# Starting the seven-product column blocks one block earlier in both feed-forward phases

## Chip, core and metric

The kernel runs on one core of a Trainium2 chip. The metric is device time in microseconds (us) of one execution. Of the kernel before there are three runs, with a median of 2231.39 us (2228.88 to 2231.76).

## The reference

One streaming-encoder layer on x of 1024 x 1024 in float32: a feed-forward phase (FFN), a mixer (banded attention beside a gated linear recurrence), and a second FFN. Each is wrapped in a norm, a modulation and a gated residual. What the change touches is the up projection of both FFNs:

```python
def swiglu(h, w_gu, w_down):            # h 1024 x 1024, w_gu 1024 x 5632, w_down 2816 x 1024
    g, u = jnp.split(h @ w_gu, 2, axis=-1)
    return (jax.nn.silu(g) * u) @ w_down
...
x = sandwich(x, ffn1, ...)
x = sandwich(x, mix, ...)
x = sandwich(x, ffn2, ...)
```

## The kernel before, in words

Every float32 matrix product is made of three matmuls on a high part and a low part of both operands (`hi` is a rounded copy made by ScalarE, `lo` the remainder, made by VectorE or GpSimd): hi·hi, hi·lo, lo·hi. One matmul is 128 x 128 weights against 512 moving columns.

**The up projection.** The 2816 columns of the gate and of the up half of `w_gu` are worked in 22 column blocks of 128 (`fb`). There are two ways to do one.

- A *plain* block (`part`, lines 453 to 455, with `cut` for the weights and `finish` for the activation) multiplies gate and up weights with the two halves of the tokens (`sh` 0 and 1), over 8 slices k of the inner dimension: 2 x 2 x 8 x 3 = 96 matmuls, of which one token half takes 48. `finish` reads the two banks (Silu on ScalarE, line 487, and the product with the up half on VectorE, line 488) and stores the result to `act_d` in device memory (line 483).
- A *seven-product* block (`block`, `product`, lines 633 to 635) does the same 2 x 2 x 2 product with seven products instead of eight, each over 4 slices: 7 x 4 x 3 = 84 matmuls. They run in the order 1, 2, 6, 5, 7, 3, 4 (`ORDER`). Products 1, 6, 7, 4 accumulate in one bank, `psX`: ScalarE has to copy the bank away after product 1 (`u`, line 649) before product 6 may go on in it, and after product 6 (`v`, line 656) before product 7 may.

**What a seven-product block needs.** Weights: `mix(fb, i)` builds the operand of product i, from sums on GpSimd (line 611), a high copy on ScalarE (line 623) and a low part on VectorE (line 624). Inside a block, the operands of the next block are made one by one in `after(i)`. Moving data: products 4, 5, 6 take sums over slices of the normed input (`hs`), made once per FFN by the generator `sums`: GpSimd adds high and low parts (`whole`, line 549, two 128 x 1024 adds for each of four slices kk), then seven VectorE instructions per kk (lines 566, 569, 573, 577, and 563 three times) and three ScalarE copies (line 559). One call of `sum_step` does one of its 17 steps. Products 3 and 7 take `differences(kk)` (lines 584 and 585, ScalarE then VectorE), which overwrite the second token half of the high and low input slices 0 to 3, so that no plain block can come after them.

**The order.** PE, VectorE, ScalarE and GpSimd each run their instructions in the order in which this hand-written program issues them; SyncE's loads and stores are placed by the scheduler. Two phases following each other may be interleaved on an engine, while each keeps its own order. `DIRECT` says with which block the seven-product blocks begin: 4 in the first FFN (`sub` 0) and 3 in the second (`sub` 2).

- First FFN: `startup` does blocks 0, 1, 2 plainly, with 16 steps of `sums` in the second token half of blocks 1 and 2. `up_phase(3)` then does block 3 plainly: its weights are cut with the low part on GpSimd, the remaining steps of `sums` are taken, and in its second token half the generator `first_needs` runs one step per k: four operands of block 4 (products 1, 2, 6, 5), four `differences`, and behind the block the other three operands (7, 3, 4).
- Second FFN: `head` does blocks 0 and 1 plainly, at the end of the mixer's output phase, with the steps of `sums` in their second token halves. `up_phase(2)` does block 2 plainly (low part on VectorE) with `first_needs` for block 3.

The temporary 128 x 512 tiles of tag `v` have two buffers (`tv`), shared by `finish` (`a`) and the two running sums of each kk (`hsum`). `raw` has three buffers, `wh` and `wl` four each, `u` three, `t4` 22. Behind the up projection, `down_phase` multiplies pairs of activation blocks with `w_down`; `all_sums` prepares its operands one step per product of a block, reading activations back from device memory for pairs that start below `direct`, and using those kept on the chip for the others.

Of the kernel before, what the change touches and what calls it, by code (L numbers as in the profile page):

```python
# [23 lines left out]
P = 128  # L24
S = 1024
D = 1024
KB = D // P
# [7 lines left out]
NEG = -1e30  # L35
HEAD_WAIT = 8
LATE = 6
FIRST_NEEDS = (1,) * 8
L_WAIT = 11
SHARE = (3, 4, 4, 5, 5)  # L40
LEFT = 40.0
GATES = (2, 0, 2, 4)
NORM_ACT = ()
DIRECT = {0: 4, 2: 3}
KEPT_FROM = 5

FIRST_HALF = (((0, 1), (), ()), ((2, 3), (0,), ()), ((), (1, 2), ()), ((), (3,), (0, 1)), ((), (), (2, 3)))
# [3 lines left out]
def kernel(  # L51
# [32 lines left out]
    def tv(name, shape=(P, 512)):  # L84
        return tmp[0].tile(list(shape), F32, tag="v", bufs=2, name=nm(name))
# [385 lines left out]
    ORDER = (1, 2, 6, 5, 7, 3, 4)  # L471

    def ffn(sub, w_gu, w_down, hh, hl, xin, xout):
# [17 lines left out]
        def load(fb, i):  # L491
            if fb >= NF or (fb, i) in wts or (fb, i) in raws:
                return
            spare = fb == 2 and sub == 0
            shape = [P, KB, P]
            if spare or fb > direct and i == 1:
                raw = t4("sr", F32, shape)
            elif fb == 1 and sub == 0:
                raw = tu("sr", F32, shape)
            else:  # L500
                raw = wpool.tile(shape, F32, tag="raw", bufs=3, name=nm("raw"))
            c0 = i * DFF + fb * P
            nc.sync.dma_start(raw, w_gu[:, c0 : c0 + P].rearrange("(k p) n -> p k n", p=P))
            raws[fb, i] = raw, spare

        def cut(fb, i):
            if (fb, i) not in raws:
                return
            raw, spare = raws.pop((fb, i))
            shape = [P, KB, P]  # L510
            if spare:
                hi, lo = t4("sh", F32R, shape), t4("sl", F32R, shape)
            else:
                hi = wpool.tile(shape, F32R, tag="wh", bufs=4, name=nm("wh"))
# [74 lines left out]
        def sum_step(n=1):  # L589
            for _ in range(n):  # L590
                next(summing, None)
# [12 lines left out]
        def mix(fb, i):  # L604
            if fb >= NF:
                return
            g, u = raws[fb, 0][0], raws[fb, 1][0]
            a, b, c, e = g[:, :4], g[:, 4:], u[:, :4], u[:, 4:]

            def pool(out, p, q, op):  # L610
                nc.gpsimd.tensor_tensor(out, p, q, op=op)  # L611

            if i == 1:
                s1 = first_sum[fb] = tv("wsum", shape=(P, 4, P))
                pool(s1, c, e, ALU.add)
                pool(c, a, c, ALU.subtract)
            s1 = first_sum[fb]
            src = {1: a, 2: b, 6: a, 5: s1, 7: c, 3: b, 4: e}[i]
            if i == 6:
                pool(a, s1, a, ALU.subtract)  # L620
            tag = ("wh", "wl")[ORDER.index(i) % 2]
            t = wpool.tile([P, 2, 4, P], F32R, tag=tag, bufs=4, name=nm("wm"))
            nc.scalar.copy(t[:, 0], src)  # L623
            nc.vector.tensor_tensor(t[:, 1], src, t[:, 0].bitcast(F32), op=ALU.subtract)  # L624
            if i == 6:
                pool(b, b, a, ALU.subtract)
            mixed[fb, i] = t
# [51 lines left out]
        def head():  # L679
            for fb in range(2):  # L680
                for k in range(KB):
                    part(fb, 0, k)
                    yield
                finish(fb, 0)
            for fb in range(2):
                for k in range(KB):
                    part(fb, 1, k)
                    sum_step()
                finish(fb, 1)

        def up_phase(started):

            for fb in range(started, direct):
                for i in range(2):
                    load(fb, i)
                    cut(fb, i)
            for i in range(2):
                load(direct, i)
            for fb in range(started, direct):
                for k in range(KB):  # L700
                    part(fb, 0, k)
                    sum_step()
                finish(fb, 0)

            def first_needs():
                sum_step(100)
                for i in ORDER[:4]:
                    mix(direct, i)
                    yield
                for kk in range(4):  # L710
                    differences(kk)
                    yield
                for i in ORDER[4:]:
                    mix(direct, i)
                    yield

            needs = first_needs()
            for fb in range(started, direct):
                for k in range(KB):
                    part(fb, 1, k)  # L720
                    if fb == direct - 1 and k < len(FIRST_NEEDS):
                        for _ in range(FIRST_NEEDS[k]):
                            next(needs)
                finish(fb, 1)
            for _ in needs:
                pass
            load(direct + 1, 0)
            load(direct + 1, 1)
            for fb in range(direct, NF):

                def after(i):
                    mix(fb + 1, i)
                    next(jobs, None)
                    if i == 3:
                        if next(early, BANK) is BANK and sub == 0:
                            raw_home[0] = "u"
                            bg(1)
                            raw_home[0] = "raw"
                    if fb == NF - 1 and i in ORDER[4:]:
                        units.fetch(ORDER[4:].index(i) + 1)  # L740

                ready[0] = fb
                block(fb, after)
                for i in range(2):
                    raws.pop((fb + 1, i), None)
                    load(fb + 2, i)
            ready[0] = NF
# [216 lines left out]
        def run(make, next_phase=None, started=0):  # L964
# [2 lines left out]
                down_phase(make, next_phase)  # L967

        return SimpleNamespace(
            run=run, load=load, cut=cut, part=part, finish=finish, sum_step=sum_step,  # L970
            fetch_raw=fetch_raw, fetch=fetch, head=head,
        )

# [591 lines left out]
    def startup(f1, hh, hl):  # L1565
# [133 lines left out]
        for k in range(KB):  # L1699
# [5 lines left out]
            if k + 3 < KB:  # L1705
                trans(1, k + 3)
        f1.finish(0, 1)
        for fb in (1, 2):
            for k in range(KB):
                f1.part(fb, 1, k)  # L1710
                f1.sum_step()
            f1.finish(fb, 1)


# [85 lines left out]
```

## Time and profile before

| what | value |
|---|---|
| runs of the kernel before | 2231.39 us median of 3, 2228.88 to 2231.76 |
| the profiled execution | 2231.5 us, its span 2229.6 us |
| mean granted clock of TensorE | 0.993 |
| busy in the span: PE, VectorE (DVE), ScalarE (ACT), GpSimd (POOL) | 97%, 60%, 46%, 34% |

The span runs from the first to the last instruction. In a row of a timeline stand start, duration, engine, line, operation, the tiles written and read, shapes and count; behind it, in brackets, the idle time of that engine just before and what ended it. PE's rows for one matmul show 0.39 us, but matmuls overlap: their starts lie closer together. A row of a table of stages has busy time and number of instructions of each engine, then the granted clock of TensorE, the DMA share and GB/s.

### The profile page before, as it was taken

Reading aid. Unit: us, or ns where it says so; the run is one execution under the profiler, and the core shown is the slowest. Engines: PE = TensorE matmul, PEld = TensorE weight load, DVE = VectorE, ACT = ScalarE, POOL = GpSimd, SP = SyncE. Lnnn points to the kernel's source line nnn. Section 1 sums busy time; section 2 is a strip of 40 time slices with the busy share of each in tenths; the row PEclk is TensorE's granted clock in tenths of the full one; section 3 lists DMA queues with packets and bytes.
Section 4 is the critical chain, followed back from the end, with each engine's and each line's share of the span. In section 5 each row is a group of like instructions: output and inputs, shape, how many; then the busy total and the mean of one; then the engine's idle time right before and its main releaser. Section 6 shows DMA issues by size and latency. Waiting matters only on the chain. (4 is left out here: it accounts for less than half of the span.)

```text
span 2229.6 us, 26752 instructions
## 1 busy us (share of the span) xinstructions
PE 2156.7 (97%) x9963; PEld 1785.0 (80%) x9963; DVE 1332.4 (60%) x1696; ACT 1016.1 (46%) x1567; POOL 758.2 (34%) x538
## 2 busy tenths in 40 slices
PE   5999999999999999999999999999999999999998
PEld 3878788888877788888898988887788788888877
DVE  6686676558356677655336666545866564544456
ACT  3533333334446678721147777436443333334443
POOL 3458885422104111100021120005658793522102
PEclk9999999999999999999999999999999999999999
DMA  9437674459575111166412011464357653348374
GB/s 294 113 120 268 226 272 153 151 183 336 182 240 184 50 50 42 57 221 221 155 40 68 26 55 54 146 199 142 110 181 263 229 209 126 113 155 275 117 230 176
DMA packets 269595, 358.36 MB, mean 161 GB/s; under 512 B 16625, under 2 KB 178585, under 8 KB 269465
## 3 DMA queue, kind: packets, MB, share of 16 engines
q1 hardware_dynamic: 256680, 310.48, 43.0%
q10 hardware_dynamic: 12784, 46.18, 5.4%
q8 instruction: 78, 1.28, 0.2%
q14 instruction: 53, 0.43, 0.1%
HBM read 265.37 MB, written 94.37 MB: 161 GB/s over the span
## 5 line engine op out<-in xcount | busy, mean ns | idle before, releaser
L624 DVE TENSOR_TENSOR wm<-raw,wm 128x512 fp32r<-128x512 f32 x152 | 161.0, 1063 | 165.3 <-ACT wm L623 162.5
L143 ACT CAST dh<-rawd 128x1024 fp32r<-128x1024 f32 x154 | 161.3, 1053 | 212.1 <-PE pv L882 67.0
L144 DVE TENSOR_TENSOR dh<-rawd,dh 128x1024 fp32r<-128x1024 f32 x130 | 161.9, 1250 | 153.4 <-ACT dh L143 145.3
L455 PE MATMUL pj<-hh,wl 128*128 128x512 f32 x576 | 228.3, 396 | 6.3 <-DVE wl L144 4.1
L454 PE MATMUL pj<-hl,wh 128*128 128x512 f32 x576 | 228.5, 397 | 5.7 <-DVE hl L336 5.7
L453 PE MATMUL pj<-hh,wh 128*128 128x512 f32 x576 | 230.9, 401 | 2.8 <-ACT h L344 1.9
L882 PE MATMUL px<-dh,dh 128*128 128x512 f32 x608 | 187.8, 390 | 1.7 <-DVE dh L144 1.7
L882 PE MATMUL pv<-dh,dh 128*128 128x512 f32 x528 | 164.3, 393 | 3.0 <-DVE dh L144 3.0
L325 POOL TENSOR_SCALAR rstd<-rstd 128x1 f32<-128x1 f32 x47 | 31.7, 675 | 392.5 <-ACT junk L324 390.9
L144 POOL TENSOR_TENSOR wl<-raw,wh 128x1024 fp32r<-128x1024 f32 x25 | 61.1, 2450 | 297.8 <-ACT wh L143 252.0
L143 ACT CAST wh<-raw 128x1024 fp32r<-128x1024 f32 (+1 forms) x86 | 86.7, 1010 | 144.9 <-DMA raw<-in_w_in_dram 41.8
L820 POOL TENSOR_TENSOR act<-act,act 128x512 f32<-128x512 f32 x54 | 87.5, 1620 | 158.9 <-DMA act<-act 89.1
L882 PE MATMUL px<-dh 128*128 128x512 f32 x352 | 137.9, 392 | 0.0
L455 PEld LDWEIGHTS pj<-hh,wl 128*128 128x128 f32 x576 | 110.2, 191 | 31.2 <-DVE wl L144 5.7
L882 PEld LDWEIGHTS px<-dh,dh 128*128 128x128 f32 x608 | 113.8, 188 | 26.5 <-DVE dh L144 3.0
L454 PEld LDWEIGHTS pj<-hl,wh 128*128 128x128 f32 x576 | 110.0, 191 | 29.9 <-DVE hl L336 7.6
L453 PEld LDWEIGHTS pj<-hh,wh 128*128 128x128 f32 x576 | 110.2, 191 | 26.2 <-ACT h L344 2.3
L144 DVE TENSOR_TENSOR wl<-raw,wh 128x1024 fp32r<-128x1024 f32 (+1 forms) x61 | 73.9, 1212 | 84.8 <-ACT wh L143 84.8
L633 PE MATMUL psX<-hh,wm 128*128 128x512 f32 x296 | 116.4, 393 | 4.3 <-ACT mixes L656 4.3
L882 PEld LDWEIGHTS pv<-dh,dh 128*128 128x128 f32 x528 | 99.5, 189 | 25.0 <-DVE dh L144 4.3
L633 PE MATMUL psX<-hs,wm 128*128 128x512 f32 x296 | 115.9, 391 | 1.6 <-ACT mixes L649 1.4
L623 ACT CAST wm<-raw 128x512 fp32r<-128x512 f32 x152 | 92.6, 613 | 52.1 <-POOL raw L611 52.0
(311 smaller groups left out, 5783.9 us busy)
## 6 DMA issues: line engine op xcount, KB each, us to landing
rawa<-in_w_ada_dram SPq DMA_DIRECT2D x56, 512.0 KB, 4.5
raw<-in_ffn_w_gu_dram SPq DMA_DIRECT2D x49, 512.0 KB, 4.7
rawd<-acts SPq DMA_DIRECT2D x88, 256.0 KB, 4.3
rawd<-downs SPq DMA_DIRECT2D x88, 256.0 KB, 4.1
raw<-in_w_in_dram SPq DMA_DIRECT2D x44, 512.0 KB, 4.0
sr<-in_ffn_w_gu_dram SPq DMA_DIRECT2D x39, 512.0 KB, 6.3
act<-act SPq DMA_DIRECT2D x37, 512.0 KB, 5.1
acts<-act ACTq DMA_DIRECT2D x36, 512.0 KB, 3.6
```

Source lines behind the costliest of these rows:

```text
L143: nc.scalar.copy(hi, raw)
L144: (eng or nc.vector).tensor_tensor(lo, raw, hi.bitcast(F32), op=ALU.subtract)
L325: nc.gpsimd.tensor_scalar(r, r, eps, None, op0=ALU.add)
L453: nc.tensor.matmul(dst, wh[:, kk, :], xhk[:, sl], start=first, stop=False)
L454: nc.tensor.matmul(dst, wh[:, kk, :], xlk[:, sl], start=False, stop=False)
L455: nc.tensor.matmul(dst, wl[:, kk, :], xhk[:, sl], start=False, stop=last)
L623: nc.scalar.copy(t[:, 0], src)
L624: nc.vector.tensor_tensor(t[:, 1], src, t[:, 0].bitcast(F32), op=ALU.subtract)
L633: nc.tensor.matmul(dst, t[:, 0, kk, :], xh, start=first and kk == 0, stop=False, skip_group_check=True)
L820: nc.gpsimd.tensor_tensor(o, p, q, op=op)
L882: nc.tensor.matmul(dst, a_[:, 0, tk], w_[:, 1, :], start=first and n == 0, stop=last and n == 2, skip_group_check=True,)
```

## The change

- `DIRECT` goes from {0: 4, 2: 3} to {0: 3, 2: 2}. The plain block of `up_phase` is gone in both FFNs: the code for it is deleted. Block 3 of the first FFN and block 2 of the second become seven-product blocks.
- `first_needs` now runs during the last plain block ahead of `up_phase`: in `startup` in the second token half of block 2, in `head` in that of block 1, one step behind each odd k (`need_step`). That gives the operands 1, 2, 6, 5. The other steps (what is left of `sums`, four `differences`, operands 7, 3, 4) are issued at the start of `up_phase`, ahead of the first seven-product block.
- `startup` takes two steps of `sums` per k in the last four k of block 1, so that 20 calls stand ahead of `up_phase` instead of 16. `head` keeps its 16; the call with which `need_step` is paired stands after `sum_step` of the same k.
- The first seven-product block's `wsum` tile moves from tag `v` to tag `u`.
- Its raw weights are loaded ahead of the last plain blocks (in the first FFN they were already loaded there).
- In the second FFN, the pair of blocks 2 and 3 is now kept on the chip for `down_phase`, not read back.

```diff
-FIRST_NEEDS = (1,) * 8
...
-DIRECT = {0: 4, 2: 3}
+DIRECT = {0: 3, 2: 2}
...
-                s1 = first_sum[fb] = tv("wsum", shape=(P, 4, P))
+                s1 = first_sum[fb] = (tu if fb == direct else tv)("wsum", shape=(P, 4, P))
...
+            for i in range(2):
+                load(direct, i)
             for fb in range(2):
                 for k in range(KB):
                     part(fb, 1, k)
                     sum_step()
+                    if fb == 1 and direct == 2:
+                        need_step(k)
                 finish(fb, 1)
 
+
+        def first_needs():
+            for i in ORDER[:4]:
+                mix(direct, i)
+                yield
+            sum_step(100)
+            for kk in range(4):
+                differences(kk)
+                yield
+            for i in ORDER[4:]:
+                mix(direct, i)
+                yield
+
+        needs = first_needs()
+
+        def need_step(k):
+            if k % 2 == 1:
+                next(needs)
+
         def up_phase(started):
 
-            for fb in range(started, direct):
-                for i in range(2):
-                    load(fb, i)
-                    cut(fb, i)
-            for i in range(2):
-                load(direct, i)
-            for fb in range(started, direct):
-                for k in range(KB):
-                    part(fb, 0, k)
-                    sum_step()
-                finish(fb, 0)
-
-            def first_needs():
-                sum_step(100)
-                for i in ORDER[:4]:
-                    mix(direct, i)
-                    yield
-                for kk in range(4):
-                    differences(kk)
-                    yield
-                for i in ORDER[4:]:
-                    mix(direct, i)
-                    yield
-
-            needs = first_needs()
-            for fb in range(started, direct):
-                for k in range(KB):
-                    part(fb, 1, k)
-                    if fb == direct - 1 and k < len(FIRST_NEEDS):
-                        for _ in range(FIRST_NEEDS[k]):
-                            next(needs)
-                finish(fb, 1)
             for _ in needs:
                 pass
             load(direct + 1, 0)
...
         f1.finish(0, 1)
+        for i in range(2):
+            f1.load(3, i)
         for fb in (1, 2):
             for k in range(KB):
                 f1.part(fb, 1, k)
-                f1.sum_step()
+                f1.sum_step(2 if fb == 1 and k >= 4 else 1)
+                if fb == 2:
+                    f1.need_step(k)
             f1.finish(fb, 1)
```

More of the change, by code (lines that the diff above doesn't have):

```diff
@@ L969, in ffn @@
         return SimpleNamespace(
-            run=run, load=load, cut=cut, part=part, finish=finish, sum_step=sum_step,
+            run=run, load=load, cut=cut, part=part, finish=finish, sum_step=sum_step, need_step=need_step,
             fetch_raw=fetch_raw, fetch=fetch, head=head,
```

## The prediction

> **What bounds the kernel now.** I read the page first, then the stages around the heads of the two FFNs, then the timelines of PE, VectorE, GpSimd and ScalarE there.
>
> ```profile
> span 2229.6 us, 26752 instructions
> PE 2156.7 (97%) x9963; PEld 1785.0 (80%) x9963; DVE 1332.4 (60%) x1696; ACT 1016.1 (46%) x1567; POOL 758.2 (34%) x538
> ```
>
> PE is busy for 97% of the span, so fewer matmuls should be time saved, if nothing else becomes late. The price of one matmul, from the chain that ended last:
>
> ```profile
> 2004.27 29.92 PE px L882 x132
> ```
>
> 29.92 / 132 = 0.2267 us from one matmul to the next. A plain block is 96 x 0.2267 = 21.8 us of PE, a seven-product block 84 x 0.2267 = 19.0. The gross gain is 12 matmuls, 2.72 us, in each FFN: 5.4 us in all. But that average hides what the removed block does besides: it covers other engines. The stages show that; columns are PE, weight loads, VectorE, ScalarE, GpSimd, then the clock.
>
> ```profile
> 92.00:116.00 24.00, 24.00 (x108) 19.87 (x107) 16.33 (x8) 4.35 (x6) 21.16 (x8) 1.00 0.19 55
> 116.00:138.00 22.00, 22.00 (x99) 18.22 (x98) 16.89 (x28) 8.11 (x14) 2.98 (x3) 1.00 0.18 61
> 1612.00:1638.00 26.00, 23.55 (x96) 19.03 (x96) 20.95 (x28) 10.02 (x18) 9.14 (x6) 0.93 0.29 91
> ```
>
> The second and third lines are the two blocks that go. PE never waits in the first of them, and VectorE runs 28 instructions in each, for 16.9 and 21.0 us. The change keeps nearly all of these and takes PE's 21.8 us away from over them. So the question is what VectorE still has to do when the last plain block ends.
>
> **First FFN: where VectorE stands.**
>
> ```profile
> 94.58 5.22 POOL L144 TENSOR_TENSOR wl<-raw,wh 128x1024 fp32r<-128x1024 f32 x2 [5.01 <-ACT wh L143]
> 112.91 2.84 POOL L549 TENSOR_TENSOR bot<-hh,hl 128x1024 f32<-128x1024 f32 x1
> 95.64 1.91 DVE L566 TENSOR_TENSOR hsum<-top 128x512 f32<-128x512 f32 x1
> 105.00 2.88 DVE L563 TENSOR_TENSOR hs<-hsum,hs 128x512 fp32r<-128x512 f32 x1
> 116.22 0.68 DVE L563 TENSOR_TENSOR hs<-bot,hs 128x512 fp32r<-128x512 f32 x1
> 116.82 0.68 DVE L566 TENSOR_TENSOR hsum<-top 128x512 f32<-128x512 f32 x1
> 127.98 0.69 DVE L569 TENSOR_TENSOR hsum<-bot,hsum 128x512 f32<-128x512 f32 x1
> 130.40 0.69 DVE L577 TENSOR_TENSOR bot<-bot,top 128x512 f32<-128x512 f32 x1
> 141.33 4.66 DVE L585 TENSOR_TENSOR hl<-bot,hh 128x512 fp32r<-128x512 f32 x4
> 137.68 0.39 PE L633 MATMUL psX<-hh,wm 128*128 128x512 f32 x1
> 144.72 0.50 PE L633 MATMUL psX<-hs,wm 128*128 128x512 f32 x1 [1.44 <-ACT mixes L649]
> 151.30 0.50 PE L633 MATMUL psX<-hh,wm 128*128 128x512 f32 x1 [0.85 <-ACT mixes L656]
> ```
>
> The seven-product blocks start at 137.68, so the last matmul of plain block 2 was due to end at 137.68 - 21.76 = 115.92. At that time VectorE is finishing the sums of the first of four slices (the instruction at 116.22 is the seventh of 28), and the last `z - x` of the sums is at 130.40. While GpSimd adds (until 112.91 + 2.84 = 115.75), a VectorE instruction takes 2.88 us; alone it takes 0.68, and starts follow each other by 0.60 (116.22 and 116.82).
>
> What moves forward: the cut of block 3 is gone, 5.22 us of GpSimd, and with it the wait of 5.01 us that stood ahead of it. In the second FFN, where no cut stands in between, GpSimd went from the first slice straight on:
>
> ```profile
> 1585.65 2.40 POOL L549 TENSOR_TENSOR bot<-hh,hl 128x1024 f32<-128x1024 f32 x1 [4.92 <-DVE hl L336]
> 1588.01 2.85 POOL L549 TENSOR_TENSOR top<-hh,hl 128x1024 f32<-128x1024 f32 x1
> ```
>
> So I take the whole 10.2 us (the other bound is 5.2). The instruction of 116.22 comes at 106.0, and that of 127.98 (the second running sum of the last slice), 11.76 later, at 117.7. One product of `finish` lies in that stretch before and after. Behind it comes `mix` for product 1, which needs that instruction's end (0.69), two copies on ScalarE queued behind each other, and its own 0.68. ScalarE's rows:
>
> ```profile
> 142.54 1.65 ACT L623 CAST wm<-raw 128x512 fp32r<-128x512 f32 x3
> 149.63 0.63 ACT L653 ACTIVATE act<-mixes 128x512 f32<-128x512 f32 x1 [4.44 <-DVE mixes L643]
> 150.17 0.60 ACT L623 CAST wm<-raw 128x512 fp32r<-128x512 f32 x1
> 150.68 0.58 ACT L656 COPY mixes<-psX 128x512 f32<-128x512 f32 x1
> ```
>
> Three copies take 1.65, so two take 1.1: the operand of product 1 is there at 117.7 + 0.69 + 1.1 + 0.68 = 120.2, and PE has been idle since 115.9. This is the wait that the change adds: 4.3 us here, before any disturbance.
>
> It is not the last. Products 1 and 2 take PE 5.4 us; product 6 waits for ScalarE's copy of `psX`, which stands in its queue behind the four `differences` and three weight copies; product 7 waits for the second copy (line 656), behind a Silu that waits for VectorE, whose queue holds four differences, three low parts, one of the next block and the add. That last chain decides. In steps of VectorE: the last `z - x` at 117.7 + 2.42 (as 127.98 to 130.40) + 1.7 (mix 1 and its wait) = 121.8; then it, mix 2, the last low part, mix 6, mix 5 and the product of `finish`, 6 x 0.60 = 3.6: the first difference at 125.5 (rounded up). From the first difference to product 7:
>
> - at least 9 x 0.60 on VectorE + 0.63 + 0.60 + 0.58 on ScalarE = 7.2 us;
> - before, with GpSimd working beside it, 151.30 - 141.33 = 9.97 us.
>
> Then products 7, 3, 4: 36 x 0.2267 = 8.16. Low end: 125.5 + 7.2 + 8.2 = 140.9. With disturbance: the four GpSimd sums of the first `mix` each hold up one VectorE instruction. Four differences took 4.66 instead of 4 x 0.60, so 0.57 each, 2.3 in all: 125.5 + 2.3 + 9.97 + 8.2 = 145.9. Before, the same point (block 4 about to start with nothing owed) is 137.68 plus the waits of 1.44 and 0.85 inside its first block: 139.97. So this FFN loses 0.9 to 5.9 us, 10.9 if GpSimd comes forward by 5.2 only. I take the middle of the first two, **+3.4**, since part of the GpSimd sums will fall into VectorE's own waits.
>
> On the disturbance the Trainium skill has a rule, "SBUF — State Buffer", section "Who interferes with whom": VectorE and GpSimd share a port pair under an exclusive lock, and an instruction with two SBUF inputs blocks until the other engine's is done. The rows of 2.88 against 0.68 agree, but 0.57 per instruction is less than a whole GpSimd instruction. By the rule taken strictly the four sums would cost up to 4 x 1.29 = 5.2 us by the row below, not 2.3, and this FFN would end at +8.8 in the disturbed case.
>
> ```profile
> 134.86 1.29 POOL L611 TENSOR_TENSOR wsum<-raw 128x512 f32<-128x512 f32 x1 [19.11 <-DMA act<-a]
> ```
>
> **Second FFN.** Here the removed block was itself late, which the change gains back.
>
> ```profile
> 1612.04 0.50 PE L453 MATMUL pj<-hh,wh 128*128 128x512 f32 x1 [0.50 <-ACT wh L143]
> 1615.17 0.50 PE L455 MATMUL pj<-hh,wl 128*128 128x512 f32 x1 [2.41 <-DVE wl L144]
> 1637.54 0.39 PE L633 MATMUL psX<-hh,wm 128*128 128x512 f32 x1
> 1609.76 1.22 DVE L144 TENSOR_TENSOR wl<-raw,wh 128x1024 fp32r<-128x1024 f32 x1
> 1610.89 0.68 DVE L563 TENSOR_TENSOR hs<-hsum,hs 128x512 fp32r<-128x512 f32 x1
> 1615.70 0.69 DVE L569 TENSOR_TENSOR hsum<-bot,hsum 128x512 f32<-128x512 f32 x1 [0.58 <-DMA act<-a]
> 1622.52 0.68 DVE L577 TENSOR_TENSOR bot<-bot,top 128x512 f32<-128x512 f32 x1
> ```
>
> Plain block 1 ends at 1612.04 - 0.50 = 1611.5; the next stretch took 26.0 us instead of 21.8 because of waits of 0.50 and 2.41 and the lower clock. The instruction at 1615.70 (third slice) waits for the store of `a` to free its buffer; `mix` 1 stands right behind it. Without the cut ahead of it (1609.76 to 1610.89, so 1.13) it comes at 1614.6 at best, at 1615.7 if the store still holds it. The last `z - x` was 6.82 later. Now mix 1 with its wait (1.7), mix 2 and mix 6 (1.2) lie in between, and behind it itself, mix 5, the product of `finish` and the last low part (2.4): first difference at 1614.6 + 6.82 + 1.7 + 1.2 + 2.4 = 1626.7, or 1627.8. Low end 1626.7 + 7.2 + 8.2 = 1642.1; disturbed 1627.8 + 2.3 + 9.97 + 8.2 = 1648.2. Before, this point is 1637.54, and no wait follows in that block. Loss 4.5 to 10.7, middle **+7.6**. PE's first wait is from 1611.5 to about 1617.
>
> **Sum.** 2231.5 (the profiled execution, 0.1 above the median of 2231.39) + 3.4 + 7.6 = **2242.5 us**. At nothing I cost: the loads (block 3's raw weights were loaded early before, too), the wsum tile in tag `u` (three buffers, free here), and the pair kept on the chip, two loads less, off the path; if its two tiles held up a `t4` buffer, that would be a wait like the one below.
>
> **Clock.** In the stage from 1612 the clock is 0.93 behind waits of 0.50 and 2.41: 26 x 0.07 = 1.8 us lost. Waits of 4 to 6 us will surely bring the same, but it falls on products 1 and 2 (and on 6 and 5), which have to wait for ScalarE's or VectorE's chain anyway, so the sum holds 0 for it, with 1.8 to 3.6 per FFN if PE ends last. The Trainium skill, "TensorE: Matmul & The Clock Gate", section "Part 1: The HAM clock gate", gives half rate after an idle window of about 3.4 us; this trace shows it behind shorter waits.
>
> **Rivals.**
>
> - *Faster: VectorE is not what ends last.* PE would only have to find operand 1 at 115.9 and 1611.5, and the gross 5.4 us would come out, plus 2.9 of the waits and 1.8 of clock in the second FFN: 2231.5 - 10.1 = 2221.4 at the utmost, 2226.1 without those. It decides itself at operand 1. For it speaks that VectorE is only 60% busy; against it that 28 sums at 0.60 and four low parts from 95.64 on already reach beyond 115.9. 6%.
> - *About the same.* Low ends in both FFNs, 5.4 us of loss, and a later wait vanishes that depends on buffers freed by stores, such as the one in the rows below with its 2.25 us and the low clock behind it (0.79 over 8 us, 1.7 us): 2231.5 + 5.4 - 4.0 = 2232.9. 16%, as the blocks' phase against `all_sums` shifts by one block.
> - *Slower by more: PE ends last after all, at half rate.* +3.6 for the two FFNs: 2246. 15%, within the range.
> - *High ends.* GpSimd forward by 5.2 only: 10.9 + 10.7 = 21.6, 2253.1. 15%.
>
> ```profile
> 1746.40 0.80 PE L633 MATMUL psX<-hh,wm 128*128 128x512 f32 x1 [2.25 <-ACT mixes L656]
> 1744.00:1752.00 8.00, 5.75 (x19) 4.48 (x19) 5.09 (x5) 3.77 (x7) 5.19 (x4) 0.79 0.31 100
> ```
>
> The forecast itself has the remaining 48%. That the change does not take the block out is excluded by `direct`, which bounds the loops.
>
> **Range and chances.** From the second rival to the high ends: 2232 to 2253. A measurement of this kernel tells about 0.2%, 4.5 us, from no change: faster is the first rival, 0.06; within 0.2% the second, 0.16; slower the rest, 0.78.
>
> **What would show it.** 24 matmuls fewer. In the first FFN a first `psX` matmul at 120 to 123 with a wait of over 4 us ended by `wm` (VectorE or ScalarE), then one at the third product ended by line 649 and one at the fifth ended by line 656; in the second FFN the same from 1611 on. First differences at 125 to 128 and 15 to 19 us behind the end of plain block 1. It is wrong if PE's waits at the two heads together stay under 5 us, or if the loss arises behind the first seven-product block.

## The result, and the profile after

| kernel | device time | runs |
|---|---|---|
| before | 2230.6 us median, 2227.78 to 2231.76 | 6 |
| after | 2253.57 us median, 2248.87 to 2256.58 | 6 |

The change makes the kernel slower: the ratio is 1.0105, with a 95% interval of 1.0094 to 1.0116, some 23 us. The forecast was 2242.5 (2232 to 2253): the sign is right and VectorE's queue is what PE waits for, but the loss is twice the one forecast, and 0.6 us beyond the range. One of the twelve executions of `second_early_halves`, further down, took 11315.71 us and is left out of its figures.

The page of after, its span and engines:

```profile
span 2253.1 us, 26756 instructions
PE 2153.9 (96%) x9939; PEld 1783.6 (79%) x9939; DVE 1345.8 (60%) x1714; ACT 1023.7 (45%) x1583; POOL 763.9 (34%) x544
```

24 matmuls fewer and 2.8 us less of PE work, in a span that is 23.5 us longer. The stages around the heads, columns as before (PE, weight loads, VectorE, ScalarE, GpSimd, clock):

```profile
92.00:118.72 26.72, 24.69 (x107) 19.93 (x107) 23.33 (x24) 7.09 (x13) 17.68 (x8) 1.00 0.03 10
118.72:148.31 29.59, 21.72 (x86) 16.59 (x86) 25.86 (x31) 13.52 (x25) 15.52 (x11) 0.88 0.52 161
1624.56:1664.41 39.85, 24.04 (x85) 18.88 (x85) 33.25 (x42) 17.85 (x33) 15.45 (x11) 0.79 0.38 119
```

The first line is the end of the plain blocks of the first FFN: VectorE runs 24 instructions there in 23.3 us, nearly 1 us each. The second line (first FFN) and the third (second FFN) run from the end of the last plain block to the end of the first seven-product block: 29.6 and 39.9 us for 84 matmuls, which are 19.0 us of PE at full rate.

Where the time goes, from the start of the same matmul in both traces:

| point | before | after | difference | change since the row above |
|---|---|---|---|---|
| first FFN: block 4 starts (before: with its own waits, 139.97) | 139.97 | 148.31 | +8.3 | +8.3 |
| first FFN: down projection starts (first `px`) | 491.01 | 504.70 | +13.7 | +5.4 |
| second FFN: plain block 1 ends | 1611.54 | 1624.56 | +13.0 | -0.7 |
| second FFN: block 3 starts | 1637.54 | 1664.41 | +26.9 | +13.9 |
| second FFN: down projection starts | 2004.11 | 2028.09 | +24.0 | -2.9 |
| end of the span | 2229.6 | 2253.1 | +23.5 | -0.5 |

The two heads (the first and the fourth row) hold 22.2 us. PE in the first FFN, with its idle time and what ended it in brackets:

```profile
92.89 0.50 PE L453 MATMUL pj<-hl,wh 128*128 128x512 f32 x1 [1.13 <-DVE hl L335]
95.67 0.50 PE L453 MATMUL pj<-hl,wh 128*128 128x512 f32 x1 [1.14 <-DVE hl L335]
...
118.49 0.39 PE L454 MATMUL pj<-hh,sl 128*128 128x512 f32 x1
124.69 0.79 PE L632 MATMUL psX<-hh,wm 128*128 128x512 f32 x1 [5.81 <-ACT wm L622]
...
133.07 0.50 PE L632 MATMUL psX<-hs,wm 128*128 128x512 f32 x1 [0.85 <-ACT mixes L648]
...
140.01 0.50 PE L632 MATMUL psX<-hh,wm 128*128 128x512 f32 x1 [1.21 <-ACT mixes L655]
...
148.31 0.39 PE L632 MATMUL psX<-hh,wm 128*128 128x512 f32 x1
```

The three waits stand where they were announced (first operand, third product, fifth product). Two more had not been: at 92.89 and 95.67 plain block 0 waits for a low part (`hl`) from VectorE. GpSimd and VectorE around them:

```profile
89.46 2.83 POOL L548 TENSOR_TENSOR top<-hh,hl 128x1024 f32<-128x1024 f32 x1
...
103.52 2.84 POOL L548 TENSOR_TENSOR bot<-hh,hl 128x1024 f32<-128x1024 f32 x1
106.32 1.74 POOL L610 TENSOR_TENSOR wsum<-raw 128x512 f32<-128x512 f32 x1
108.14 1.62 POOL L610 TENSOR_TENSOR raw<-raw,raw 128x512 f32<-128x512 f32 x1
```

```profile
87.89 4.94 DVE L335 TENSOR_TENSOR hl<-h,hh 128x512 fp32r<-128x512 f32 x2
...
100.05 1.25 DVE L568 TENSOR_TENSOR hsum<-bot,hsum 128x512 f32<-128x512 f32 x1 [1.56 <-DMA act<-a]
...
104.04 2.88 DVE L572 TENSOR_TENSOR bot<-bot,hsum 128x512 f32<-128x512 f32 x1
106.84 1.78 DVE L562 TENSOR_TENSOR hs<-hsum,hs 128x512 fp32r<-128x512 f32 x1
108.54 1.77 DVE L576 TENSOR_TENSOR bot<-bot,top 128x512 f32<-128x512 f32 x1
110.24 0.68 DVE L562 TENSOR_TENSOR hs<-bot,hs 128x512 fp32r<-128x512 f32 x1
...
119.05 0.68 DVE L584 TENSOR_TENSOR hl<-bot,hh 128x512 fp32r<-128x512 f32 x1
...
122.78 0.69 DVE L568 TENSOR_TENSOR hsum<-bot,hsum 128x512 f32<-128x512 f32 x1
...
134.11 1.18 DVE L584 TENSOR_TENSOR hl<-bot,hh 128x512 fp32r<-128x512 f32 x1
```

From 101 to 110 the two engines go in step: each of VectorE's instructions starts 0.4 to 0.5 us behind one of GpSimd's and ends 0.5 to 0.6 us behind it. Beside an add of 128 x 1024 it takes 2.88, beside one of 128 x 512 1.77, and alone, from 110.24 on, 0.68. So the adds set VectorE's pace, and the two adds of `mix` 1 prolong this by 3.4 us, for two instructions that take 1.2 alone. In before these two adds waited 19.11 us for a store of `a` (the row at 134.86), which had to free a buffer of tag `v` for `wsum`; with `wsum` in tag `u` they follow at once. No run moves the tag alone.

The second FFN, PE first, then GpSimd, VectorE and ScalarE:

```profile
1624.33 0.39 PE L454 MATMUL pj<-hh,wl 128*128 128x512 f32 x1
1632.71 0.79 PE L632 MATMUL psX<-hh,wm 128*128 128x512 f32 x1 [8.00 <-ACT wm L622]
...
1648.08 0.80 PE L632 MATMUL psX<-hs,wm 128*128 128x512 f32 x1 [7.82 <-ACT mixes L648]
...
1656.23 0.40 PE L632 MATMUL psX<-hh,wm 128*128 128x512 f32 x1
```

```profile
1620.74 1.62 POOL L610 TENSOR_TENSOR raw<-raw,raw 128x512 f32<-128x512 f32 x1
1633.52 1.60 POOL L610 TENSOR_TENSOR raw<-wsum,raw 128x512 f32<-128x512 f32 x1 [11.16 <-issue]
1637.77 1.61 POOL L610 TENSOR_TENSOR raw<-raw 128x512 f32<-128x512 f32 x1 [2.65 <-DVE wm L623]
1644.55 1.59 POOL L610 TENSOR_TENSOR wsum<-sr 128x512 f32<-128x512 f32 x1 [5.17 <-ACT hs L558]
1646.21 1.60 POOL L610 TENSOR_TENSOR sr<-raw,sr 128x512 f32<-128x512 f32 x1
```

```profile
1630.80 0.69 DVE L568 TENSOR_TENSOR hsum<-bot,hsum 128x512 f32<-128x512 f32 x1 [1.56 <-DMA act<-a]
1632.69 0.69 DVE L623 TENSOR_TENSOR wm<-raw,wm 128x512 fp32r<-128x512 f32 x1 [1.20 <-ACT wm L622]
...
1641.92 0.69 DVE L623 TENSOR_TENSOR wm<-raw,wm 128x512 fp32r<-128x512 f32 x1 [1.20 <-ACT wm L622]
...
1644.93 1.75 DVE L562 TENSOR_TENSOR hs<-bot,hs 128x512 fp32r<-128x512 f32 x1
1646.61 1.75 DVE L623 TENSOR_TENSOR wm<-wsum,wm 128x512 fp32r<-128x512 f32 x1
...
1648.89 2.48 DVE L584 TENSOR_TENSOR hl<-bot,hh 128x512 fp32r<-128x512 f32 x4
```

VectorE reaches the first differences only at 1648.89, 24.3 us behind the end of plain block 1 (15 to 19 had been announced). Here the first and the third product wait, but not the fifth. PE's second long wait is for ScalarE's copy of `psX`, which in program order stands behind the casts of the sums and operands, and so behind VectorE. The adds at 1644.55 and 1646.21 are those of the *next* block's `mix` 1: GpSimd had nothing else to do and took them early, into VectorE's critical stretch.

In the first FFN's later blocks, ScalarE and its DMA queue, then PE:

```profile
229.98 0.48 ACTq L792 DMA_DIRECT2D downs<-bot  x1
237.98 0.63 ACT L652 ACTIVATE act<-mixes 128x512 f32<-128x512 f32 x1 [7.46 <-DMA downs<-bot]
```

```profile
239.65 0.50 PE L632 MATMUL psX<-hh,wm 128*128 128x512 f32 x1 [2.11 <-ACT mixes L655]
```

A Silu waits 7.46 us for a store of rebuilt down weights to land, apparently because its new `act` tile has been given that tile's buffer; behind it in ScalarE's queue stands the copy that PE needs. PE's wait is one of four in after from 201 to 287 us (1.26, 2.11, 2.08, 2.36), where before had 1.21 and 1.85 from 268 to 273.

### The profile page after: what moved, and what is told of

It reads as the page before. It is cut to its first block, busy times and chain, and to the rows that moved or that the text cites. A ratio compares the mean times of both kernels' runs of the same rounds, so it can differ in the third digit from the quotient of the medians.

```text
span 2253.1 us, 26756 instructions
## 1 busy us (share of the span) xinstructions
PE 2153.9 (96%) x9939; PEld 1783.6 (79%) x9939; DVE 1345.8 (60%) x1714; ACT 1023.7 (45%) x1583; POOL 763.9 (34%) x544
## 4 chain that ended last, share of the span: by engine, by line
PE 70%; DVE 6%; ACT 5%; DMA 3%; POOL 2%; issue 2%; SPq 0%; ACTq 0%; DVEq 0%; POOLq 0%
PE pv L872 8%; PE px L872 7%; PE pj L454 6%; PE pj L452 6%; PE pj L453 6%; PE psX L632 5%; PE psX L633 5%; PE psX L634 5%; PE pj L1218 4%; PE psZ L632 3%; PE psZ L634 3%; PE psZ L633 3%; PE pv L1265 1%; PE psY L632 1%; PE psY L634 1%
## 5 line engine op out<-in xcount | busy, mean ns | idle before, releaser
L623 DVE TENSOR_TENSOR wm<-raw,wm 128x512 fp32r<-128x512 f32 x160 | 166.5, 1043 | 170.4 <-ACT wm L622 170.1
L453 PE MATMUL pj<-hl,wh 128*128 128x512 f32 x512 | 202.1, 395 | 8.0 <-DVE hl L335 8.0
L452 PE MATMUL pj<-hh,wh 128*128 128x512 f32 x512 | 204.6, 400 | 3.5 <-ACT h L343 3.5
L454 PE MATMUL pj<-hh,wl 128*128 128x512 f32 x512 | 201.7, 394 | 3.2 <-DVE wl L143 1.7
L143 POOL TENSOR_TENSOR wl<-raw,wh 128x1024 fp32r<-128x1024 f32 x23 | 55.9, 2435 | 293.8 <-ACT wh L142 249.3
L632 PE MATMUL psX<-hh,wm 128*128 128x512 f32 x312 | 124.1, 398 | 19.2 <-ACT wm L622 13.8
L632 PE MATMUL psX<-hs,wm 128*128 128x512 f32 x312 | 123.1, 395 | 8.7 <-ACT mixes L648 8.7
L633 PE MATMUL psX<-hl,wm 128*128 128x512 f32 x312 | 123.3, 395 | 0.0
L634 PE MATMUL psX<-hh,wm 128*128 128x512 f32 x312 | 123.0, 394 | 0.0
L633 PE MATMUL psX<-hs,wm 128*128 128x512 f32 x312 | 122.4, 392 | 0.0
L634 PE MATMUL psX<-hs,wm 128*128 128x512 f32 x312 | 122.4, 392 | 0.0
L453 PEld LDWEIGHTS pj<-hl,wh 128*128 128x128 f32 x512 | 97.4, 190 | 30.1 <-DVE hl L335 10.7
```

The source lines that it names most:

```text
L143: (eng or nc.vector).tensor_tensor(lo, raw, hi.bitcast(F32), op=ALU.subtract)
L452: nc.tensor.matmul(dst, wh[:, kk, :], xhk[:, sl], start=first, stop=False)
L453: nc.tensor.matmul(dst, wh[:, kk, :], xlk[:, sl], start=False, stop=False)
L454: nc.tensor.matmul(dst, wl[:, kk, :], xhk[:, sl], start=False, stop=last)
L632: nc.tensor.matmul(dst, t[:, 0, kk, :], xh, start=first and kk == 0, stop=False, skip_group_check=True)
L633: nc.tensor.matmul(dst, t[:, 0, kk, :], xl, start=False, stop=False, skip_group_check=True)
```

## The experiments

**Each FFN alone.** The plain block goes in one FFN only; in the other the code of before stays (the lines are shown against before).

```diff
-DIRECT = {0: 4, 2: 3}
+DIRECT = {0: 3, 2: 3}
```

> The change in the first FFN alone; the second keeps its plain block 2. Theory Q (VectorE's queue of sums and operands ends last at each head, now that no plain block covers it): the first FFN's head costs what it did in the changed kernel, +8.3 us until block 4 starts, and 2239 to 2246 us in all, the rest being waits further back. Rival L (the loss comes from later waits on buffers and stores, as the blocks' phase against all_sums has shifted): the head costs under 3 us, and the total follows the waits behind it.

Measured: 2240.89 us (2239.31 to 2245.7), ratio 1.0064 [1.0045, 1.0082].

```diff
-DIRECT = {0: 4, 2: 3}
+DIRECT = {0: 4, 2: 2}
```

> The change in the second FFN alone. Theory Q: +13.9 us from the end of plain block 1 to the start of block 3, 2241 to 2247 us in all; with the first FFN alone it adds up to the whole change (+23 us) within 4 us. Rival L: the two do not add up, because each shifts the other's waits.

Measured: 2241.38 us (2239.57 to 2241.62), ratio 1.0061 [1.0046, 1.0076]. With 2228.51 for before on that chip the two lose 12.4 and 12.9, 25.3 together, near the 23 of the whole: each FFN pays by itself. The first FFN's head alone costs 7.7 us (8.3 in after), and the second's takes 39.8 us, as in after.

**Sums of one slice only.** The 21 VectorE instructions of the slices 1 to 3, and six of the eight adds, are left out, and with them nine ScalarE copies, in each FFN; the products take slice 0's sums four times, so the result is not the reference's. Once on after, once on before.

```diff
             for kk in range(4):
+                if kk:
+                    for i in (4, 5, 6):
+                        hs[i, kk] = hs[i, 0]
+                    dif[kk] = dif[0]
...
+                    continue
```

> The changed kernel with the sums made for one slice of four only; the other three use the first one's tiles, so 21 of 28 VectorE and 6 of 8 GpSimd instructions of the sums are left out, and the output is not the reference's. Theory Q: PE's first wait at each head shrinks from 5.8 and 8.0 us to under 1 us, and this kernel is 5 to 10 us faster than the kernel before with the same sums left out (5.4 us of matmuls, and the late cut in the second FFN). Rival L: it stays over 5 us slower than that one.

> The kernel before with the same sums left out (one slice of four made, its tiles used for all). Theory Q: its plain block covered the sums, so 2224 to 2231 us: only the waits of 2.3 us in block 4 and up to 4.7 us around the late cut can go. Rival L says the same of this one; it is the measure for the kernel beside it.

Measured: after with one slice 2210.85 us, ratio to the kernel before 0.9926 [0.9907, 0.9945]; before with one slice 2216.36, ratio 0.9948 [0.9931, 0.9965], lower than expected, as the sums were no free work in before either. After less before is now -5.5 us by the medians and -4.9 by the ratios, with some 6 us of doubt either way, near the gross gain of the 24 matmuls (5.4). The traces are more exact: there is no wait at either head of after (product 1 follows the plain block without a gap, and the first seven-product block takes 19.04 us in both FFNs). So the loss at the heads hangs on the sums, that is on VectorE's instructions, the adds and the copies together. Most of the later loss goes too: behind its head the first FFN has one wait of 3.1 us left, beside 2.1 and 1.1 in before with one slice.

**No adds on GpSimd.** `whole` copies the high part on ScalarE in place of adding high and low on GpSimd, in after and in before.

```diff
-                        nc.gpsimd.tensor_tensor(dst, hh[k].bitcast(F32), hl[k].bitcast(F32), op=ALU.add)
+                        nc.scalar.copy(dst, hh[k].bitcast(F32))
```

> The changed kernel without the eight adds on GpSimd that rebuild the input from its parts: ScalarE copies the high part instead, so the low part is left out of the sums. VectorE's queue keeps its 28 sums. Theory Q with the shared port as its largest mis-sized term: 4 VectorE instructions of the first FFN took 9.0 us instead of 2.4, 6 of the second took 14.0 instead of 3.6, and PE lost 2.3 us to low parts of plain block 0, so 15 to 19 us come back: 2234 to 2240 us, against 2253.6. If the port mattered little and the number of instructions decides, under 6 us come back.

> The kernel before, with the eight adds of GpSimd in each FFN that rebuild the normed input (two of 128 x 1024 for each slice) replaced by ScalarE copies of the high part alone: the low part is left out of the sums. In the changed kernel the same edit gave back 20 us. Theory (the adds lock VectorE out, and that costs only where no plain block covers it): nothing to speak of here, 2226 to 2231 beside 2228 to 2231 for the kernel before. Rival (the adds are dear wherever they stand, and the change has only little to do with it): 2210 to 2221.

Measured: on after 2233.68 us, ratio 1.0026 [1.0016, 1.0037], 0.3 below the expected range; on before 2220.34, ratio 0.9968 [0.9957, 0.9979]. Here my theory missed: I had held that the adds cost nothing under a plain block, but before gets back some 9 us too, 3.6 of it at its first head (the waits of 1.44 and 0.85 are gone) and 4.2 at its second (21.8 us from plain block 1 to block 3 instead of 26.0). By the ratios the change costs 1.0026 - 0.9968 = 0.58%, 13 us, without the adds, and 23 with them; the 13 have some 3 us of doubt, and the heads of the two traces differ by 4.3 and 7.7, 12.0 together. So about 10 of the 23 us are VectorE held up by these eight adds, in a place where nothing covers it any more. The other 13 are not the queues of VectorE and ScalarE alone: the sums of `mix` on GpSimd still hold VectorE, in the second head four instructions, at 1.75 to 1.78 us instead of 0.68. How the 13 split is not shown. (The eight copies burden ScalarE, so 13 is, if anything, too much.) After without adds, PE:

```profile
1625.85 0.80 PE L632 MATMUL psX<-hs,wm 128*128 128x512 f32 x1 [7.46 <-ACT mixes L648]
```

The first operand is now in time in the second FFN, but the third product waits nearly as long as in after (7.82): ScalarE's copy of `psX` stands behind all sums.

**PE kept busy.** 86 matmuls on a spare bank fill the idle time of both heads, 28 in the first FFN and 58 in the second.

```diff
+            if fb == direct:
+                filler(FILL[sub][0])
             run(1, chain, True)
...
+            if fb == direct:
+                filler(FILL[sub][1])
             run(6, chain, False)
...
+FILL = {0: (20, 8), 2: (30, 28)}
```

> The changed kernel with 86 further matmuls, whose results nobody uses, in PE's idle time at the heads: 20 and 8 in the first FFN, 30 and 28 in the second, ahead of products 1 and 6 of the first seven-product block (19.5 us of PE at full clock). Theory Q (PE waits for VectorE and ScalarE, and its low clock there is hidden): within 2 us of the changed kernel, 2251.5 to 2255.5. Rival C (half rate after the idle time ends last): 3 to 5 us faster. If PE itself ended last, up to 19 us slower.

Measured: 2251.36 us (2248.87 to 2254.2), ratio 1.0103 [1.0084, 1.0123], 0.1 below the expected range. The stages of the heads:

```profile
118.56:148.27 29.71, 26.87 (x113) 20.63 (x112) 26.06 (x33) 13.56 (x25) 15.62 (x11) 1.00 0.49 159
1618.28:1659.76 41.48, 35.56 (x143) 27.35 (x142) 33.95 (x45) 17.86 (x33) 17.03 (x12) 0.96 0.37 114
```

19.5 us more of PE work, the clock at 1.00 and 0.96 instead of 0.88 and 0.79, and the heads take 29.7 and 41.5 us, no less than the 29.6 and 39.9 of after. PE and its clock are not on the path of the heads.

**Another order.** Operands 1 and 2 ahead of the second half of the sums, all sums ahead of operands 6 and 5, differences and the last operands behind the first copy of `psX`. The weight sums of `mix` 1 now come with operand 6, and in this block the Silu stands behind the second copy.

```diff
-            for i in ORDER[:4]:
-                mix(direct, i)
-                yield
+            mix(direct, 1)
+            mix(direct, 2)
+            yield
             sum_step(100)
+            mix(direct, 6)
+            yield
+            mix(direct, 5)
+            yield
             for kk in range(4):
                 differences(kk)
...
                 def after(i):
+                    if fb == direct and i in (1, 2):
+                        next(needs)
                     mix(fb + 1, i)
```

> The changed kernel in another order: operands 1 and 2 ahead of the later sums, all sums ahead of operands 6 and 5, and the differences and the last three operands behind the first copy of psX, not ahead of it. The same instructions. Theory Q: PE starts product 1 without a wait, and ScalarE's copy no longer holds product 6, but product 6 still waits for the sums: 4 to 6 us less per FFN, 2242 to 2247 us. If only the length of VectorE's queue counted and no order in it, nothing changes.

Measured: 2248.3 us (2245.96 to 2249.17), ratio 1.0087 [1.0070, 1.0105]; it gains 4 us by the ratios and 5 by the medians, of the 8 to 12 expected. PE in the first and in the second FFN:

```profile
130.97 0.80 PE L632 MATMUL psX<-hs,wm 128*128 128x512 f32 x1 [6.27 <-ACT mixes L648]
```

```profile
1629.47 0.80 PE L632 MATMUL psX<-hh,wm 128*128 128x512 f32 x1 [7.55 <-ACT wm L622]
```

In the first FFN the wait has only moved from the first product to the third; in the second it still stands at the first. The order decides mainly where PE waits; by itself it takes away little of the waiting.

**The adds made early.** With that order, the second token half of the rebuilt input is written straight into its tile when it is made, only the first half is added (half the GpSimd work), and earlier; the weight sums of the first seven-product block go to VectorE, so that GpSimd does not hold it up.

```diff
-        h32 = tv("h32")
+        h32 = home(k)[:, sl] if home and sh == 1 else tv("h32")
...
+        def half(k):
+            nc.gpsimd.tensor_tensor(home(k)[:, h1], hh[k][:, h1].bitcast(F32), hl[k][:, h1].bitcast(F32), op=ALU.add)
...
-                nc.gpsimd.tensor_tensor(out, p, q, op=op)
+                (nc.vector if fb == direct else nc.gpsimd).tensor_tensor(out, p, q, op=op)
...
+            if j >= 6:
+                for k in range(4):
+                    f1.half((j - 6) * 4 + k)
             if j == 7:
                 h_lo(1, 0, h_act(1, 0, True))
```

> The reordered kernel with VectorE's queue relieved: the second token half of the rebuilt input is written once where it is made, instead of being added up again on GpSimd, the first half is added up earlier (eight adds of half the size, ahead of the sums), and the first block's weight sums run on VectorE. The result is the reference's. Theory Q: the 28 sums run at 0.6 us each from 95 us on, PE hardly waits at either head, and the gross 5.4 us come out together with the waits that the kernel before has there (2.3, 2.9 and 1.8): 2214 to 2226 us. Rival L: not under 2230.

Measured: 2232.81 us (2230.62 to 2234.25), ratio 1.0020 [1.0010, 1.0029]: 19 us better than after by the ratios and 21 by the medians, but short of the expected 2214 to 2226. The second FFN's head does what was expected (23.5 us from the end of plain block 1 to block 3, against 26.0 before and 39.9 after). The first has a new wait, long before its head. GpSimd, VectorE and PE:

```profile
68.04 8.36 POOL L549 TENSOR_TENSOR whole<-hh,hl 128x512 f32<-128x512 f32 x6
```

```profile
63.30 1.67 DVE L249 SCALAR_TENSOR_TENSOR acc<-rawa,c_act,acc 128x256 f32<-128x256 f32 x4
...
68.35 5.53 DVE L249 SCALAR_TENSOR_TENSOR acc<-rawa,c_act,acc 128x256 f32<-128x256 f32 x4
```

```profile
77.00 0.80 PE L453 MATMUL pj<-hl,wh 128*128 128x512 f32 x1 [5.32 <-DVE hl L335]
```

The six early adds meet four small VectorE instructions of the start, which take 5.53 us instead of 1.67, and PE waits 5.32 us for the low part behind them: the same cause in a new place.

**The second FFN alone, with early adds.** The first FFN as in before, the second as in `early_halves` (the line is shown against before).

```diff
-DIRECT = {0: 4, 2: 3}
+DIRECT = {0: 4, 2: 2}
```

> The first FFN as in the kernel before (seven-product blocks from block 4); in the second they begin at block 2, with the order and the early halves of the run early_halves. Theory (what the change pays in the second FFN is VectorE locked out by GpSimd's adds, and once they are made earlier one block less is worth its price): the head takes 23 to 24 us from the end of plain block 1 to the start of block 3 instead of 26.0, the wait of 2.25 us near 1746 stays away, and the whole takes 2221 to 2227. Rival (what the head gains is given back in the blocks behind it): 2229 to 2234.

Measured: 2224.36 us (2222.58 to 2227.92), ratio 0.9985 [0.9976, 0.9993], as expected. The head takes 23.3 us, of which one wait is 2.11, for the third operand:

```profile
1620.60 0.60 PE L645 MATMUL psX<-hs,wm 128*128 128x512 f32 x1 [2.11 <-ACT wm L635]
```

The wait near 1746 is 0.63. So with VectorE relieved, one block less costs nothing against before. That the block less brings the gain is not shown: before with early halves was not run, and before without its adds gets 9 us back with the block in place.

**The first FFN's adds on VectorE.** As `early_halves`, with the first FFN's eight half adds on VectorE, four in the second token half of plain block 0 and four between the sums.

```diff
-            nc.gpsimd.tensor_tensor(home(k)[:, h1], ...
+            (nc.vector if sub == 0 else nc.gpsimd).tensor_tensor(home(k)[:, h1], ...
```

> The run early_halves with one difference: in the first FFN the eight half adds are not on GpSimd near 70 us but on VectorE, four during plain block 0's second token half and four between the sums. Theory (the wait of 5.32 us on hl at 77.00, and the half rate around it, come from VectorE being locked out by GpSimd's half adds): no wait over 1 us before the end of plain block 2, which ends at 116 to 118 instead of 124.10; whole 2222 to 2228. Rival (VectorE is simply full there, whoever adds): plain block 2 ends on time, but PE then waits 4 us or more at the first operand or the third product, whole 2230 to 2236.

Measured: 2225.69 us (2223.45 to 2230.44), ratio 0.9993 [0.9984, 1.0002]; 7 us better than `early_halves`. Plain block 2 ends at 115.93 without a wait. PE then waits 1.49 and 1.03, and block 4 starts at 139.65:

```profile
123.01 0.50 PE L643 MATMUL psX<-hs,wm 128*128 128x512 f32 x1 [1.49 <-ACT wm L633]
...
124.77 0.50 PE L645 MATMUL psX<-hs,wm 128*128 128x512 f32 x1 [1.03 <-DVE wm L634]
```

VectorE runs eight instructions more here, without GpSimd's adds beside it, and is earlier. But the down projection of the first FFN starts at 495.73, against 491.01 before: the later waits are still there.

**Stores one step sooner.** As the run above, with the stores that ScalarE issues one step behind their job instead of two.

```diff
-                while ending and (hurry or ending[0][0] + 2 <= n):
+                while ending and (hurry or ending[0][0] + 1 <= n):
```

> The run halves_on_vectore with one number changed: the stores of the rebuilt down weights and activations, which ScalarE issues two steps behind the last GpSimd operation of their job, are issued one step behind it. Theory (the later waits of the first FFN, 2.14 us at 229.83, 2.07 at 252.85, 2.16 at 278.10, come from the new tile act or mixes taking the buffer of a tile whose store to device memory was issued 8 us before and has not landed, as ScalarE's row at 228.16 with its 7.49 us says): with stores some 2.7 us sooner at least two of the three waits fall below 0.5 us, and the whole takes 2218 to 2223. Rival (ScalarE's queue then waits for GpSimd at the issue, or the phase just shifts): waits of the same sum elsewhere, 2224 to 2229.

Measured: 2223.41 us (2220.53 to 2225.7), ratio 0.9974 [0.9965, 0.9983], 0.4 above the expected bound. The down projection of the first FFN starts at 488.24, 7.5 us sooner, 6.8 of it won in the blocks behind the head. Of the waits at 229.83, 252.85 and 278.10, which were over 2 us each, one is left, and longer:

```profile
248.87 0.50 PE L643 MATMUL psX<-hh,wm 128*128 128x512 f32 x1 [3.23 <-ACT mixes L667]
```

So in this version the later loss of the first FFN (5.0 us in the run above) comes mostly from stores that land late in buffers that are wanted again, as far as one execution of each tells. In the span only 1.8 of the 7.5 us are left: the stretch from there to the second FFN's first seven-product block takes 2.4 us longer, its blocks 2.0, and its down projection 1.3. What causes that was not followed up. This version is faster than both kernels, by 0.26% than before; how before itself would fare with early adds and sooner stores was not run.

## Why the prediction was right in sign and wrong in size

- **The bound.** "The question is what VectorE still has to do when the last plain block ends": right. With one slice of sums nothing is lost at the heads, and the gross 5.4 us come out as 5.5 (4.9 by the ratios; the closeness is more than the runs can tell).
- **Clock and PE.** Taken at 0, since they fall on waits that end elsewhere: right, as the heads of the filled run show. The rival in which PE ends last is refuted.
- **First head, +3.4 forecast, +8.3 measured.** The step that failed is "I take the whole 10.2 us (the other bound is 5.2)". The last slice's second running sum was to come 10.2 us sooner than 127.98, at 117.7, and came at 122.78, 5.2 sooner: 5.1 us of error, where the head is off by 4.9. GpSimd's adds do end 9.4 us sooner (106.36 instead of 115.75), but VectorE does not move with them. Its first instruction in step with them, at 100.05, waits for a store of `a`, as the one at 102.50 in before did:

```profile
102.50 2.58 DVE L569 TENSOR_TENSOR hsum<-bot,hsum 128x512 f32<-128x512 f32 x1 [4.95 <-DMA act<-a]
```

That is 2.5 us sooner only, so by the end of the adds VectorE has done less of its work. Then the two adds of `mix` 1 hold two more of its instructions, and it comes free at 110.24 instead of 116.22, 6.0 sooner. The text put `wsum` in tag `u` at nothing; without the wait for tag `v` these adds came forward. For the bound of 5.2 the text gave only its high end, 10.9; by its own steps that bound gives 5.9 to 10.9, around the measured 8.3. From that sum to product 7 (line 655's wait, at 140.01) it took 17.2 us, within the text's 15.0 to 20.1, though not in the text's order: three of the four differences ran ahead of `mix` 1, from 119.05 on. The waits at 92.89 and 95.67, 2.3 us, were not in the text: GpSimd, without its 5 us wait for block 3's cut, reaches the adds while VectorE still owes plain block 0 its low parts. They delay VectorE as well (its product of `finish` comes at 97.20 instead of 95.03), but how much of the 8.3 they make is not shown, as PE waits for VectorE later anyway.
- **Second head, +7.6 forecast, +13.9 measured.** Two steps failed. The third slice's second sum was to stand 3.1 to 4.2 us behind the end of plain block 1 and stands at 1630.80 - 1624.56 = 6.2. Its row waits for the store of `a`, as the text allowed, but VectorE's product for that store came only at 1627.35, and the two adds of `mix` 1 had held two VectorE instructions ahead of it at 1.78. From there to the first difference the text has 12.1 us, and 2.3 more for GpSimd at the high end; it took 18.1. Of that, 4.4 are four VectorE instructions held up by GpSimd, 1.1 each instead of 0.57, two of them by adds of the next block, which the text had not looked for; and 1.3 is a second wait for ScalarE, at `mix` 6, where the text had one at `mix` 1 only. The last step, from the first difference to block 3, was 15.4 at its low end and took 1664.41 - 1648.89 = 15.5.
- **"0.57 each".** Taken from four differences that took 4.66 us in before, as if GpSimd had worked beside all four. GpSimd's rows of before at that time:

```profile
141.49 1.68 POOL L611 TENSOR_TENSOR wsum<-sr 128x512 f32<-128x512 f32 x1 [1.23 <-DVE wm L624]
143.25 1.60 POOL L611 TENSOR_TENSOR sr<-raw,sr 128x512 f32<-128x512 f32 x1
```

Two adds, so two instructions paid: (4.66 - 4 x 0.60) / 2 = 1.1 each, which is what the rows of after show. The Trainium skill's rule ("SBUF — State Buffer", section "Who interferes with whom"), that an instruction with two inputs blocks until the other engine's is done, agrees with these rows and with those of 1.77 beside 1.62 to 1.74. What VectorE pays is the rest of the add it meets, some 1.1 us, not the whole. The text put the first head at +8.8 by whole adds; that this lies near 8.3 is luck, as it keeps the 10.2 us that failed.

- **Behind the heads.** The text has nothing for the first FFN and, in a rival, a gain of up to 4.0 where a later wait vanishes. In the second FFN that wait did vanish, and 2.9 us were gained. In the first 5.4 were lost. That they go to stores whose buffers are wanted sooner is what the row at 237.98 suggests and the last run shows for another version; all 5.4 are not shown to be that. The size also varies: the same stretch is 2.4 us longer than in before in the filled run, and 8.2 in the first FFN alone.
- **A reading that does not hold.** "28 sums at 0.60 and four low parts from 95.64 on already reach beyond 115.9": 95.64 + 32 x 0.60 = 114.8. It is the waits for stores and the slow instructions beside the adds that carry VectorE beyond.
- **What would have been a sign against it**, a loss behind the first seven-product block, is thus true of 5.4 us of 23.

So the rival whose number came true is *high ends* (2253.1), though not for its reason: GpSimd was early, but VectorE was not. The closeness is luck: it had 10.9 and 10.7 us at the heads, where 8.3 and 13.9 were measured, and nothing behind them.

## What to carry to other kernels

Work of an engine that costs nothing under a matmul block gets its price when the block goes: count the queue's instructions from the moment at which the cover ends, and price each at what it takes beside the other engine's work of that time, not alone and not at a mean. When a wait is taken away from GpSimd, ask which of its next instructions come forward, and into which stretch of VectorE. Another order alone gave 4 to 5 us of 23; with it, the rest came from less work on GpSimd beside VectorE at that time: halves written where they are made, and adds on the engine that needs the result. And before counting such a cure for the change, try it on the kernel before: that was not done here.

## What was not expected of the hardware

- A VectorE instruction with two inputs in SBUF and a GpSimd add go in step, one for one: VectorE's 128 x 512 takes 2.88 us beside adds of 128 x 1024, 1.77 beside adds of 128 x 512, and 0.68 alone. Smaller ones lose nearly as much each: four of 128 x 256 beside adds of 128 x 512 took 5.53 instead of 1.67 us. GpSimd loses less, 2.84 instead of 2.40 and 1.62 to 1.74 instead of 1.29.
- So moving the adds *to* VectorE made VectorE earlier: eight half adds more, and the first FFN's first seven-product block ends at 139.65 instead of 144.34.
